# A hybrid decoder step whose opening is rewritten as one list of 370 steps over all engines

## The chip, the cores and the metric

The kernel runs on one core of a Trainium2 chip. The metric is the device time of one execution in microseconds (us), as the median over several runs. TensorE (PE) does matrix products and transposes into the accumulation banks of PSUM; VectorE (DVE), ScalarE (ACT) and GpSimd (POOL) work element by element; SyncE (SP) and ACT issue the transfers (DMAs) of this kernel, each on a queue of its own. Every engine works through its own list of instructions in order, and the engines wait for each other through semaphores.

## The reference, cut to what matters

One layer of a decoder: 1024 prompt rows and 8x8 sample rows, 1024 channels. Cut to the part that the opening of the kernel touches:

```
shift, scale, gate = jnp.split(jax.nn.silu(c) @ w_ada + b_ada, 3, axis=-1)
h = rmsnorm(x, norm_g) * (1 + scale[:, None]) + shift[:, None]
proj = h @ w_in
u_pool, z_pool, z_ssm, xbc, dt_raw, g_raw = jnp.split(proj, SPLITS, axis=-1)
dt = jax.nn.softplus(dt_raw + dt_bias)
gates = jax.nn.sigmoid(g_raw)
...
m = gates[..., :D_MODEL] * p + gates[..., D_MODEL:] * s
x = x + gate[:, None] * (m @ w_o)
```

Behind this follow a pooling branch, a state space branch (convolution, scan over chunks, gated norm), two output projections, and the final norm.

## The kernel before

**The whole.** h is kept transposed in SBUF, eight channel tiles k of 128 channels by T = 1088 columns (1024 prompt, 64 sample), as a high and a low part, `hh_[k]` (float32r) and `hl_[k]` (the rest), so that a product takes three matmuls: high by high, low weight by high, high weight by low. Most of w_in is multiplied in pairs of 128-column tiles by a seven-product Strassen-Winograd scheme (`strassen`, line 654, each product two halves of 12 matmuls 128x272). It needs sums of the h tiles (S1 to S4, made by `combine`, line 507, in place in `tf`) and of the weights (`pair_w`, line 556, through `split`, line 165: ACT writes `whi`, DVE or POOL writes `wlo`).

**The opening**, `first` (line 898), goes up to the end of the first such pair. The 1088 columns are taken as three blocks `BLK` of 256, 384 and 448 columns, made from x tiles 0-1, 2-4 and 5-8 (x tile 8 holds the 64 sample rows). For each block: load the x tiles; sum of squares of each (`x_square`, L204); a square root (L215) and a reciprocal (L219); `x_unit` (L224) scales an identity by it, and `x_spread` (L226) multiplies that by ones on PE, so that the row factors stand along columns in `rsb`; `x_turn` (L255) transposes each channel tile on PE, and `x_out` (L270) multiplies the transposed tile by `rsb` into `tf[k]`: for even k by DVE, for odd k by a copy on ACT (L275) and a multiply on POOL (L276). `c_silu`, `c_turn` and the `ada_...` functions (L299-L335) make shift and scale, in four parts p of two channel tiles each: 32 small matmuls (L305), a copy, a transpose (L320), and adds into `md`. `h_make` (L337) makes the two parts of h of one block from `tf` and `md`. `products` (L914) multiplies two tiles of gate columns (kept in `gs_d`, L924 the matmul) by block and by pairs of channel tiles; `dt_block` (L770) multiplies the dt columns; `gate_mm` (L879) the eight 512 KB rows of w_ada for gate. `warm(n)` (L246) puts n matmuls of ones on PE, whose results nobody reads.

**What sets the order.** `in_line` (L368) chains every instruction of each engine in the order in which the program writes it, for all five engines (SP with its loads among them). So the order inside `first` is the order of its calls; the tags and buffer numbers of the pools only add waits (a load into a buffer waits until its old content has been read). PE stands in it as follows: transposes of all three blocks, then from L924 on `products` in the order of blocks 0, 1, 2 for k = 0-1, then 2-3, 4-5, 6-7, with ada parts between; the gate rows 0-3 behind blocks 0 and 1 of the last k; the dt blocks; gate rows 4-7; then the fourteen half products of Strassen (L643). Behind the opening the units of the other pairs follow, with instructions placed by a scheduler.

Of the kernel before, what the change touches and what calls it, by code (L numbers as in the profile page):

```python
# [46 lines left out]
def tile_pool_ssd_step(  # L47
# [100 lines left out]
    def c_silu():  # L148
        act(c9, c9, AF.Silu)
        act(rs[:, 0:1], eps, AF.Sqrt)  # L150

    def c_turn():
        ps = PB()
        for k in range(KT):
            nc.tensor.transpose(ps[:, k * 9:k * 9 + 9], c9[:, k * P:(k + 1) * P], ident[:9, :9])
        V.tensor_copy(scT[:, :, 0:9], ps[:, :72].rearrange("p (k b) -> p k b", b=9))

    def v_turn():
        ps = PB()
        nc.tensor.transpose(ps[:, :44], vb, ident[:44, :44])  # L160
        V.tensor_copy(vT, ps[:, :44])
        V.tensor_scalar(vT[:, 8:16], vT[:, 8:16], 1.0, None, ALU.add)


# [25 lines left out]
    xr = []  # L190
# [8 lines left out]
    def x_load(i):  # L199
        n = P if i < 8 else NS  # L200
        xt = R([P, D]) if i == 8 else xbig[i // 4][:, i % 4, :D]
        load(xt[:n], x_prompt[0, i * P:(i + 1) * P, :] if i < 8 else x_sample.rearrange("b t d -> (b t) d"))
        xr.append((xt, n))

    def x_square(i, eng):
        xt, n = xr[i]
        sqj = pa.tile([P, D], F32, tag="rawA", name=nm("sqj"), bufs=3)
        if eng is V:
            V.scalar_tensor_tensor(sqj[:n], xt[:n], 1.0, xt[:n], ALU.mult, ALU.mult, accum_out=ss[:n, i:i + 1])
        else:  # L210
            act(sqj[:n], xt[:n], AF.Square, accum_out=ss[:n, i:i + 1])

    def x_root(a, b):
        n = xr[a][1]
        act(rs[:n, a:b], ss[:n, a:b], AF.Sqrt, bias=eps[:n], scale=1.0 / D)  # L215

    def x_unit(a, b):
        n = xr[a][1]
        V.reciprocal(rs[:n, a:b], rs[:n, a:b])  # L219
        if not dg:  # L220
            dg.append(R())
        for i in range(a, b):
            n = xr[i][1]
            V.tensor_scalar(dg[0][:n, i * P:i * P + n], ident[:n, :n], rs[:n, i:i + 1], None, ALU.mult)  # L224
# [3 lines left out]
    turns, turned = [0], []  # L228

    def x_spread(g3, eng):  # L230

        pr = PB()
        c = 0
        for i in range((0, *XG)[g3], XG[g3]):
            n = xr[i][1]
            mm(pr[:, c:c + n], ones[:n, :], dg[0][:n, i * P:i * P + n], start=True, stop=True)
            c += n
        o = BLK[g3][0]
        if eng is V:
            V.tensor_copy(rsb[:, o:o + c], pr[:, :c])  # L240
        else:
            act(rsb[:, o:o + c], pr[:, :c], AF.Copy)

    beat = []

    def warm(n):  # L246

        if not beat:
            beat.append(PC())
        for _ in range(n):  # L250
            mm(beat[-1][:, 256:256 + P], ones, ones, start=True, stop=True)

    def x_turn(g3, *ks):

        banks = []  # L255
        for k in ks:
            if g3 == 0:
                tf[k] = tfp.tile([P, T], F32, tag="tf", name=nm("tf"), bufs=8)
            banks.append((PA if turns[0] % 2 else PB)())
            turns[0] += 1  # L260
        c = 0
        for i in range((0, *XG)[g3], XG[g3]):
            xt, n = xr[i]
            for k, px in zip(ks, banks):
                nc.tensor.transpose(px[:, c:c + n], xt[:n, k * P:(k + 1) * P], ident[:n, :n])
            c += n
        turned.extend((g3, k, px, c) for k, px in zip(ks, banks))

    def x_out(n=1):
        for _ in range(n):  # L270
            g3, k, px, c = turned.pop(0)
            o = BLK[g3][0]
            t, r = tf[k][:, o:o + c], rsb[:, o:o + c]
            if k % 2:
                act(t, px[:, :c], AF.Copy)  # L275
                nc.gpsimd.tensor_tensor(t, t, r, ALU.mult)  # L276
            else:
                V.tensor_tensor(t, px[:, :c], r, ALU.mult)
# [20 lines left out]
    def ada_mm(part, k):  # L299
        a, b = PARTS[part]  # L300
        n = (b - a) * P // 2
        if k == 0:
            pm[part] = PC() if part else beat[0]
        for j in range(4):
            mm(pm[part][32 * j:32 * j + 32, :n], scT[:, k, :], wraw[part, k][:, j // 2, j % 2 * n:j % 2 * n + n],  # L305
               start=(k == 0), stop=(k == KT - 1))

    def ada_out(part):
        a, b = PARTS[part]
        n = (b - a) * P // 2  # L310
        mr = pa.tile([P, 256], F32, tag="rawA", name=nm("mr"), bufs=3)
        act(mr[:, :n], pm[part][:, :n], AF.Copy)
        return mr

    def ada_end(part, mr):
        a, b = PARTS[part]
        ni = (b - a) // 2
        ps = PB()
        for i in range(ni):
            nc.tensor.transpose(ps[:, i * P:(i + 1) * P], mr[:, i * P:(i + 1) * P], ident)  # L320
        pv = ps[:, :ni * P].rearrange("p (i j b) -> p j i b", i=ni, j=4)
        for s in (1, 0):
            m = slice(8 * s + a, 8 * s + b)
            V.tensor_tensor(md[:, m].rearrange("p (j i) b -> p j i b", i=ni), pv[:, 2 * s:2 * s + 2, :, 0:9],
                            vT[:, m].rearrange("p (j i) -> p j i", i=ni).unsqueeze(3).to_broadcast([P, 2, ni, 9]), ALU.add)
            if s:
                V.tensor_tensor(md[:, m], md[:, m],
                                vT[:, 16 + a:16 + b].unsqueeze(2).to_broadcast([P, b - a, 9]), ALU.mult)

# [6 lines left out]

    def h_make(g3, ks):  # L337

        o, w = BLK[g3]
        e = min(o + w, SEQ) - o  # L340

        def low(k):
            V.tensor_tensor(hl_[k][:, o:o + w], tf[k][:, o:o + w], hh_[k][:, o:o + w].bitcast(F32), ALU.subtract)
        for k in ks:
            if hh_[k] is None:
                hh_[k], hl_[k] = h_tile(k, 0), h_tile(k, 1)
            t = tf[k][:, o:o + w]
            hi = hh_[k][:, o:o + w]
            sc, sh = md[:, 8 + k], md[:, k]
            if e == w:  # L350
                act(hi, t, AF.Identity, scale=sc[:, 0:1], bias=sh[:, 0:1])
            if k % 2:
                act(t[:, :e], t[:, :e], AF.Identity, scale=sc[:, 0:1], bias=sh[:, 0:1])
            else:
                V.tensor_scalar(t[:, :e], t[:, :e], sc[:, 0:1], sh[:, 0:1], ALU.mult, ALU.add)
            if e < w:
                ts_ = t[:, e:w].rearrange("p (b i) -> p b i", i=8)
                V.tensor_tensor(ts_, ts_, sc[:, 1:9].unsqueeze(2).to_broadcast([P, NB, 8]), ALU.mult)
                V.tensor_tensor(ts_, ts_, sh[:, 1:9].unsqueeze(2).to_broadcast([P, NB, 8]), ALU.add)
# [1933 lines left out]
```

## Time and profile before

| | |
|---|---|
| median of three runs | 1270.49 us (1265.09 to 1270.58) |
| profiled execution | 1269.77 us |
| span of its trace, first to last instruction | 1268.1 us |
| mean granted TensorE clock over the span | 0.996 |
| PE busy in the span | 98% |
| DVE, POOL, ACT busy | 77%, 57%, 54% |
| the opening's PE work | from 1.07 us to about 105 us |

The profiled execution lies 0.72 us under the median, and its span 1.67 us under its own time. Rows of the profile are read so: a timeline row has the start in us, the duration, the engine, the line of the kernel, the operation, what it writes <- what it reads, the number of like instructions in a row, and in brackets how long the engine stood idle before it and what ended that. An fp32 matmul of the program stands as two or more in the trace. PEclk is the share of its full clock that TensorE was granted.

### The profile page before, as it was taken

How to read it: one execution, taken by the hardware profiler on the slowest of the kernel's cores; microseconds unless marked ns; L12 is line 12 of the kernel's file. 1: busy time of each engine (PE TensorE's matmuls, PEld its weight loads, DVE VectorE, ACT ScalarE, POOL GpSimd, SP SyncE). 2: the span in 40 equal slices, each digit the busy share in tenths (PEclk: the TensorE clock that was granted, in tenths of full speed). 3: DMA queues.
4: the chain of work that ended last, by engine and by line, in shares of the span. 5: the costliest groups of instructions: out<-in, count | busy, mean ns of one | idle time of the engine just before them, and what ended most of it. 6: DMA issues, size and time to landing. Idle time of an engine off the chain costs nothing.

```text
span 1268.1 us, 26648 instructions
## 1 busy us (share of the span) xinstructions
PE 1247.2 (98%) x9775; PEld 1164.8 (92%) x9775; DVE 978.2 (77%) x1715; ACT 682.3 (54%) x1570; POOL 727.5 (57%) x621
## 2 busy tenths in 40 slices
PE   9999999999999999999999999999999999999997
PEld 8779999999999999999989999998898888899885
DVE  5786689986998588876676775488687898659986
ACT  5665347465556546455655554645676655401425
POOL 4106767786868777764444444355686877503662
PEclk9999999999999999999999999999999999999999
DMA  9836454565546455444656565998888887766884
GB/s 323 248 134 207 148 158 149 183 199 162 162 157 197 161 156 176 132 148 121 175 168 192 175 184 156 317 317 266 254 247 284 285 242 256 267 215 218 250 194 155
DMA packets 264675, 257.99 MB, mean 203 GB/s; under 512 B 29889, under 2 KB 204561, under 8 KB 264538
## 3 DMA queue, kind: packets, MB, share of 16 engines
q1 hardware_dynamic: 183808, 163.93, 42.3%
q10 hardware_dynamic: 78434, 88.18, 20.1%
q0 software_dynamic: 2304, 4.20, 1.8%
q8 instruction: 77, 1.26, 0.4%
q14 instruction: 52, 0.43, 0.1%
HBM read 171.26 MB, written 85.10 MB: 202 GB/s over the span
## 4 chain that ended last, share of the span: by engine, by line
PE 65%; DVE 3%; DMA 2%; issue 1%; POOL 1%; ACT 1%; SPq 0%; ACTq 0%; POOLq 0%; DVEq 0%
PE mm L387 17%; PE mm L643 14%; PE ps L643 14%; PE ps L1284 2%; PE pc L643 2%; PE pc L1606 2%; PE ps L1287 2%; PE ps L2088 2%; PE ps L2090 2%; PE ps L2089 2%; DMA xb<-xbc 2%; PE ps L1581 1%; PE ps L1374 1%; PE ps L1397 1%; PE mm L2098 1%
## 5 line engine op out<-in xcount | busy, mean ns | idle before, releaser
L171 POOL TENSOR_TENSOR wlo<-rawA,whi 128x512 fp32r<-128x512 f32 x120 | 172.5, 1441 | 158.7 <-ACT whi L168 100.8
L171 POOL TENSOR_TENSOR wlo<-raw,whi 128x512 fp32r<-128x512 f32 x94 | 155.3, 1661 | 96.6 <-ACT whi L168 89.7
L387 PE MATMUL mm<-Y,whi 128*128 128x352 f32 (+1 forms) x960 | 197.2, 335 | 0.3 <-DVE Y L1644 0.3
L387 PEld LDWEIGHTS mm<-Y,whi 128*128 128x128 f32 x960 | 160.1, 189 | 6.6 <-issue 4.8
L1127 DVE SCALAR_TENSOR_TENSOR GA<-GA,cvT,GA 128x1112 f32<-128x1112 f32 x72 | 132.1, 1839 | 0.1
L643 PE MATMUL mm<-Y,whi 128*128 128x272 f32 x832 | 125.3, 292 | 3.0 <-ACT whi L168 2.1
L643 PE MATMUL ps<-Y,whi 128*128 128x272 f32 x832 | 123.3, 291 | 0.0
L168 ACT ACTIVATE whi<-raw 128x512 fp32r<-128x512 f32 x96 | 59.5, 628 | 109.8 <-DVE raw L575 48.6
L643 PEld LDWEIGHTS mm<-Y,whi 128*128 128x128 f32 x832 | 112.2, 188 | 6.2 <-ACT whi L168 2.2
L168 ACT ACTIVATE whi<-rawA 128x512 fp32r<-128x512 f32 x125 | 78.0, 626 | 72.9 <-PE ps L643 39.5
L643 PEld LDWEIGHTS ps<-Y,whi 128*128 128x128 f32 x832 | 111.8, 189 | 0.4
L1272 ACT ACTIVATE dec<-dec,acT 128x128 f32<-128x128 f32 (+1 forms) x288 | 86.9, 383 | 25.4 <-POOL dec L1263 24.3
L387 PE MATMUL mm<-Y,wlo 128*128 128x352 f32 (+1 forms) x480 | 99.4, 329 | 0.0
L387 PEld LDWEIGHTS mm<-Y,wlo 128*128 128x128 f32 x480 | 82.3, 189 | 0.0
L463 POOL TENSOR_TENSOR pw<-pw,ph 128x512 fp32r<-128x512 f32 x40 | 68.9, 1722 | 14.3 <-ACT ph L461 14.0
L643 PE MATMUL mm<-G,whi 128*128 128x272 f32 x496 | 73.6, 290 | 0.0
L643 PE MATMUL ps<-G,whi 128*128 128x272 f32 x496 | 72.6, 288 | 0.0
L643 PE MATMUL ps<-Y,wlo 128*128 128x272 f32 x416 | 69.6, 289 | 0.0
L643 PE MATMUL mm<-Y,wlo 128*128 128x272 f32 x416 | 69.5, 289 | 0.0
L643 PEld LDWEIGHTS mm<-G,whi 128*128 128x128 f32 x496 | 66.9, 189 | 0.7
L643 PEld LDWEIGHTS ps<-G,whi 128*128 128x128 f32 x496 | 66.3, 188 | 0.0
L1543 POOL TENSOR_TENSOR Y<-xb,Y 128x512 fp32r<-128x512 f32 x32 | 41.6, 1301 | 38.1 <-ACT Y L1541 38.1
(545 smaller groups left out, 3230.9 us busy)
## 6 DMA issues: line engine op xcount, KB each, us to landing
rawA<-in_w_in SPq DMA_DIRECT2D x62, 512.0 KB
dec<-acs_d SPq DMA_DIRECT2D x32, 512.0 KB
xbc<-GA ACTq DMA_DIRECT2D x24, 512.0 KB
Y<-wo SPq DMA_DIRECT2D x10, 1024.0 KB
pw<-in_w_ssm_out ACTq DMA_DIRECT2D x32, 256.0 KB
ws<-ph ACTq DMA_DIRECT2D x32, 256.0 KB
ws<-pw ACTq DMA_DIRECT2D x32, 256.0 KB
h<-in_state_ssm SPq DMA_DIRECT2D x32, 256.0 KB
```

The costliest lines, as they stand in the source:

```text
L168: ins = act(hi[:, :, :ncols], raw[:, :, :ncols], AF.Copy)
L171: (eng or nc.gpsimd).tensor_tensor(lo[:, :, :ncols], raw[:, :, :ncols], hi[:, :, :ncols].bitcast(F32), ALU.subtract)
L387: mm(ps[:, :n], w[k // 4][h][:, k % 4, :], r[k][:, o:o + n], start=(j == 0), stop=(j == len(terms) - 1))
L463: nc.gpsimd.tensor_tensor(raw.bitcast(F32R), raw, hi.bitcast(F32), ALU.subtract)
L643: mm(p, w[j // 8][:, k], A(k, s)[j // 4 == 1], start=(j == 0), stop=(j == 11))
L1127: V.scalar_tensor_tensor(d[:, :n], rp[:, k:k + n], cvT[:, 24 * k + mc:24 * k + mc + 1], d[:, :n], ALU.mult, ALU.add)
L1272: act(dec[:, h], dec[:, h], AF.Exp, bias=acT[:S, c, 8 * g + h:8 * g + h + 1], scale=-1.0)
L1284: mm(o[hh], xd[:S, 2 * q + hh, :], dec[:S, 2 * q + hh], start=True, stop=state is None)
L1287: mm(o[hh], state[:, h * 64:h * 64 + 64], cE[:, h], start=False, stop=True)
L1543: nc.gpsimd.tensor_tensor(yl[g][:, :, o:o + S], v, yhc.bitcast(F32), ALU.subtract)
L1606: mm(pu, bt, xw.rearrange("p h d -> p (h d)"), start=True, stop=True)
L2088: mm(ps, hi, y[:, k, c0:c0 + cw], start=(first and k == 0), stop=False)
```

## The change

The closures of the opening (`c_silu`, `c_turn`, `v_turn`, the `x_...`, `ada_mm`, `ada_out`, `ada_end`, `h_make`, `combine`, `gate_mm`, `gate_end`, and the early variants in `pair_w` and `strassen`) are gone. In their place `first` walks through `ORDER1`, a list of 370 words; each word is one step of one engine, with a letter where several engines could do it (V, A, G for DVE, ACT, POOL). `in_line` chains all five engines as before, and behind the opening the instructions stand in the order of before.

```
+    ORDER1 = """
+        warm6 sq0.A silu sq1.V turn0.0 turn0.6 turn0.7 turn0.5 turn0.2 cturn tab sq2.V vturn warm2 sct root0
+        sq8.V sq3.A turn0.1 warm8 unit0.V sq4.A vt spread0 root1 rsb0.A ada0.0 unit1.V ada0.2 out0.0 out0.1
...
+        pr0.6 t0.7.A wl1.V gt0 h2.7 l0.7.V gt2 wl0.V gt4 l1.6.V pr0.7 l2.6.V pr1.6 sgt ca2.V pr2.6 l2.7.V
...
+    """.split()
...
+        free, held, said = ["B", "A", "B", "A", "B", "A", "B"], {}, set()
+        def bank(key):
+            p = free.pop(0)
+            held[key] = (PA() if p == "A" else PB(), p)
+            return held[key][0]
...
+        def out(g, k):
+            o, w = BLK[g]
+            V.tensor_tensor(tf[k][:, o:o + w], give(("turn", g, k))[:, :w], rsb[:, o:o + w], ALU.mult)
...
+        def warm(n):
+            if pm[0] is None:
+                t = beat[0]
+            elif len(free) > 1:
+                t = bank("warm")
+                give("warm")
+            else:
+                return
...
+        def gt(k0):
...
+            for k in (k0 + 4, k0 + 5):
+                if k < KT:
+                    gate_load(k)
...
-        for i in range(9):
-            x_load(i)
+        x_load(8, store_)
...
+        for word in ORDER1:
...
+            calls[name](*args)
+            said.add(".".join(f for f in fs if f.isdigit() or f == fs[0]))
+            loads()
```

In words: the seven PSUM banks go round in a list, and a bank comes back when the step that reads it is written. The 24 `out` steps are one DVE multiply each (before: 12 on DVE, 12 as an ACT copy and a POOL multiply). Of the squares, DVE does x tiles 1, 2, 8 and 6 and ACT the rest (before: DVE 0, 1, 3, 5, 8). `warm` does nothing when fewer than two banks are free; 16 matmuls of the program are left of 43 written before. `pr b.k` is one channel tile k of block b (6 matmuls, before 12 for two tiles), from block 1 on. Loads come from a list that is emptied as far as its conditions are met. Their order on SP is x tiles 0-4, ada part 0, two weight tiles, x tiles 5-7, the other ada parts; x tile 8 goes on ACT's queue. Gate row k + 4 is loaded by the step that multiplies gate row k, into its buffer.

**ACT's first instructions.** R_116 holds c; vb the vectors b_ada, norm_g, ssm_norm_g, pool_scale; R_224 is x tile 8 (after); ss and rs the sums of squares and their roots. Before:

```order
L140 DMA vb<-in_norm_g 8x128
L141 DMA vb<-in_ssm_norm_g 16x128
L142 DMA vb<-in_pool_scale 4x128
L149 ACTIVATE R_116<-R_116 9x1024
L150 ACT_TABLE_LOAD
L150 ACTIVATE rs<-eps 128x1
L215 ACTIVATE rs<-ss,eps 128x2
```

After, in the same place:

```order
L140 DMA vb<-in_norm_g 8x128
L141 DMA vb<-in_ssm_norm_g 16x128
L142 DMA vb<-in_pool_scale 4x128
L185 DMA R_224<-in_x_sample 64x1024
L673 ACTIVATE sqj_279,ss<-Y_129 128x1024
L722 ACTIVATE R_116<-R_116 9x1024
L725 ACT_TABLE_LOAD
L725 ACTIVATE rs<-eps 128x1
L677 ACTIVATE rs<-ss,eps 128x2
```

The load of x tile 8 and the square of x tile 0 now stand ahead of silu (the ACTIVATE on R_116).

**DVE's first instructions after the change.** tf is h before shift and scale, vT the transposed vectors, R_339 the scaled identities, R_224 x tile 8.

```order
L671 SCALAR_TENSOR_TENSOR sqj_282,ss<-Y_129 128x1024
L671 SCALAR_TENSOR_TENSOR sqj_314,ss<-Y_129 128x1024
L733 COPY scT<-mm_304 128x8x9
L671 SCALAR_TENSOR_TENSOR sqj_322,ss<-R_224 64x1024
L681 RECIPROCAL rs<-rs 128x2
L688 TENSOR_SCALAR R_339<-ident,rs 128x128 x2
L739 COPY vT<-ps_316 128x44
L740 TENSOR_SCALAR vT<-vT 128x8
L681 RECIPROCAL rs<-rs 128x3
L688 TENSOR_SCALAR R_339<-ident,rs 128x128 x3
L718 TENSOR_TENSOR tf_284<-ps_285,rsb 128x256
```

The square of x tile 8 (R_224) has moved ahead of the first reciprocal; before it was DVE's seventeenth instruction, behind the multiplies of blocks 0 and 1.

**PE at the gate rows.** pc_963 (after: pc_919) is the accumulator, scT the transposed silu(c); the R and gk tiles are rows of w_ada. Before, rows 2 and 3 with their neighbours (rows 0 and 1, R_811 and R_813, stand one group of 12 products earlier, and rows 4 to 7 behind the dt blocks):

```order
L924 MATMUL mm_609<-G_930,whi_756 128x384
L924 MATMUL ps_610<-G_930,whi_760 128x384
L883 MATMUL pc_963<-R_815,scT 32x256 x4
L883 MATMUL pc_963<-gk_817,scT 32x256 x4
L924 MATMUL ps_674<-G_925,whi_756 128x448
```

After, rows 0 to 5 in one piece:

```order
L844 MATMUL ps_762<-G_868,whi_709 128x256
L882 MATMUL pc_919<-R_677,scT 32x256 x4
L882 MATMUL pc_919<-R_679,scT 32x256 x4
L882 MATMUL pc_919<-R_681,scT 32x256 x4
L882 MATMUL pc_919<-gk_827,scT 32x256 x4
L882 MATMUL pc_919<-R_928,scT 32x256 x4
L882 MATMUL pc_919<-R_930,scT 32x256 x4
L844 MATMUL mm_761<-G_871,whi_654 128x256
```

R_928 and R_930 (gate rows 4 and 5) take the buffers of R_677 and R_679 (rows 0 and 1), so that their loads start when PE has read those; between the last reading and the need stand the eight matmuls of rows 2 and 3.

783 lines of the change are left out of this document (351 added, 432 removed).

## The prediction

> **What bounds the kernel now.** I read the page first, then the waits of PE in the opening, then the timeline of PE, and then the rows of the engines that PE waits for. The page:
>
> ```profile
> span 1268.1 us, 26648 instructions
> PE 1247.2 (98%) x9775; PEld 1164.8 (92%) x9775; DVE 978.2 (77%) x1715; ACT 682.3 (54%) x1570; POOL 727.5 (57%) x621
> ```
>
> PE is idle for 21 us of the whole span, so the kernel ends when PE's work ends, and the opening matters as far as it lets PE start late or wait. The waits of PE up to 105 us (us in total, times, the longest):
>
> ```profile
> PE mm L643 <- ACT whi L168: 2.1, 1, 2.1
> PE mm L924 <- ACT G L351: 1.2, 2, 1.0
> ...
> PE mm L924 <- ACT Y L351: 1.0, 1, 1.0
> PE mm L643 <- DVE Y L513: 0.9, 2, 0.6
> ```
>
> These are what an order could take away: 5.2 us. The timeline of PE places them:
>
> ```profile
> 30.38 1.00 PE L924 MATMUL mm<-Y,whi 128*128 128x256 f32 x4 [0.97 <-ACT Y L351]
> ...
> 79.70 1.28 PE L643 MATMUL mm<-Y,whi 128*128 128x272 f32 x8 [2.13 <-ACT whi L168]
> ...
> 81.48 2.02 PE L643 MATMUL ps<-Y,whi 128*128 128x272 f32 x8
> ...
> 84.20 1.33 PE L643 MATMUL mm<-G,whi 128*128 128x272 f32 x8
> ...
> 85.88 1.17 PE L643 MATMUL ps<-G,whi 128*128 128x272 f32 x8
> ...
> 88.87 1.16 PE L643 MATMUL ps<-G,whi 128*128 128x272 f32 x8
> ...
> 90.38 1.16 PE L643 MATMUL mm<-Y,whi 128*128 128x272 f32 x8
> ...
> 106.85 1.18 PE L643 MATMUL ps<-G,whi 128*128 128x272 f32 x8
> ```
>
> The first product starts at 30.38; before it PE only has transposes, small matmuls and warm-up, and waits for DVE, ACT and POOL. The row at 106.85 is my mark: the first G product of the next pair, with all of the opening and two half products of that pair behind it, before and after the change. A half product takes 1.51 us (88.87 to 90.38), but the one at 79.70 took 1.78, the next 2.72 and the third 1.68. The windows say why:
>
> ```profile
> 77.70:81.10 3.40, 1.40 (x11) 1.40 (x12) 1.93 (x3) 2.59 (x6) 0.00 (x0) 1.00 0.18 65
> 81.10:84.50 3.40, 3.40 (x18) 3.40 (x17) 3.38 (x6) 2.64 (x6) 0.00 (x0) 0.50 0.18 67
> ```
>
> In the first stretch PE (first busy column) worked 1.40 of 3.40 us, and in the next its clock was 0.50. So the wait of 2.13 us cost a second time: 0.27 + 1.21 + 0.17 = 1.65 us.
>
> **The change part by part.** I follow PE from its first product to the mark. Before, this took 106.85 - 30.38 = 76.47 us, of which the waits behind the first product are 1.2 (G) + 2.13 + 0.9 = 4.2 and the half clock 1.65; PE's own work is 70.6 us. The sum after is: start of the first product, plus this work as it is now, plus new waits.
>
> *What is taken away, 5.9 us.* The products now stand by single tiles, the dt blocks and the rest of the products stand between the first Strassen halves, and the weights' high parts (`wh0`, `wh1`) are written some 25 words ahead of the first half that reads them. In the old order ACT's list has `whi` behind the copies of two dt blocks. I take all 4.2 us of waits and the 1.65 us of half clock as gone, and put 0.2 us of short new waits in their place.
>
> *Work that moves behind the first product, +0.25 us.*
>
> ```profile
> 15.38 0.27 PE L265 MATMUL ps<-ident,Y 128*128 128x128 f32 x1
> 15.49 0.27 PE L265 MATMUL mm<-ident,Y 128*128 128x128 f32 x1
> ...
> 21.68 1.30 PE L236 MATMUL ps<-R,ones 128*128 128x128 f32 x8
> ...
> 32.40 1.08 PE L305 MATMUL pc<-G,scT 128*32 128x128 f32 x32
> 33.41 0.45 PE L924 MATMUL mm<-Y,whi 128*128 128x384 f32 x1
> ```
>
> Four turns of block 2 with four transposes each come later: 16 x 0.11 = 1.75 us. Three quarters of ada part 1 (24 of the program's matmuls; 16 of them are the 32 of the row at 32.40, 1.01 us) come earlier: -1.5 us.
>
> *Warm-up, 0.* The program has 43 warm-up matmuls before and 16 after (twice that in the trace). All stand ahead of the first product, where PE waits for others anyway; nothing is gained. What they cover is the clock there; that is a bound below.
>
> *The start of the first product, +0.3 us.* This is DVE's chain now, since DVE has all 24 `out` multiplies. The rows of one group each:
>
> ```profile
> L276 POOL TENSOR_TENSOR tf<-tf,rsb 128x256 f32<-128x256 f32 (+2 forms) x12 | 12.0, 1018 | 15.3 <-ACT tf L275 12.4 <-DVE rsb L240 2.9
> L278 DVE TENSOR_TENSOR tf<-ps,rsb 128x256 f32<-128x256 f32 (+2 forms) x12 | 5.9, 528 | 0.4 <-ACT rsb L242 0.4
> L275 ACT ACTIVATE tf<-mm 128x256 f32<-128x256 f32 (+2 forms) x12 | 5.1, 467 | 0.0
> ```
>
> For 5.9 us more on DVE, POOL loses 12.0 and ACT 5.1. The chain starts with x tile 8, whose square stands ahead of everything on DVE:
>
> ```profile
> 4.91 1.23 DVE L209 SCALAR_TENSOR_TENSOR sqj<-Y 128x1024 f32<-128x1024 f32 x1 [4.91 <-DMA Y<-in_x_prompt]
> ...
> 6.30 1.23 DVE L209 SCALAR_TENSOR_TENSOR sqj<-Y 128x1024 f32<-128x1024 f32 x1 [0.16 <-DMA Y<-in_x_prompt]
> ...
> 8.74 0.48 DVE L224 TENSOR_SCALAR R<-ident,rs 128x128 f32<-128x128 f32 x2
> ...
> 10.42 1.49 DVE L278 TENSOR_TENSOR tf<-ps,rsb 128x256 f32<-128x256 f32 x4
> ...
> 15.44 1.49 DVE L278 TENSOR_TENSOR tf<-ps,rsb 128x384 f32<-128x384 f32 x3 [0.37 <-ACT rsb L242]
> 16.92 1.22 DVE L209 SCALAR_TENSOR_TENSOR sqj<-R 64x1024 f32<-64x1024 f32 x1
> ...
> 27.66 0.85 DVE L162 TENSOR_SCALAR vT<-vT 128x8 f32<-128x8 f32 x1
> ...
> 30.36 0.41 DVE L355 TENSOR_SCALAR tf<-tf,md 128x256 f32<-128x256 f32 x1 [0.67 <-ACT Y L351]
> 30.81 0.42 DVE L343 TENSOR_TENSOR Y<-tf,Y 128x256 fp32r<-128x256 f32 x1
> ```
>
> When does x tile 8 land? On ACT's queue it follows five small loads:
>
> ```profile
> 2.15 0.33 ACTq L140 DMA_DIRECT2D vb<-in_norm_g  x1
> ...
> 4.82 0.32 ACTq L141 DMA_DIRECT2D vb<-in_ssm_norm_g  x1
> 5.22 0.28 ACTq L142 DMA_DIRECT2D vb<-in_pool_scale  x1
> 5.55 1.06 ACT L149 ACTIVATE R<-R 9x1024 f32<-9x1024 f32 x1 [2.33 <-DMA R<-in_c_sample]
> ```
>
> The load issued at 4.82 followed one issued at 2.15, so issues are held up there by over 2 us; x tile 8 goes out between 5.5 and 8. The first x tile (512 KB) was there 4.1 us after its issue at 0.8, and the next 1.39 us later; with half the bytes at half the rate beside SP's loads it is 4.1 us again. So it lands between 9.6 and 12.1; from above I have only 16.92, where DVE reads it today without a wait. I take 12.0, by the held issue. Silu then starts not at 5.55 but behind that issue and a square, near 9, and scT is there at 11, which is ahead of 12.
>
> From 12.0 DVE has, up to the reciprocal of block 2: two squares 2.4; three reciprocals and md's three small steps, each at most an identity's 0.24, 1.3 in all; five scaled identities 1.2; vT 0.45 (its 0.85 of today stands beside a POOL multiply that goes; bounds 0.24, the identity's, and 0.85; I stay near the lower one); seven outs of 256 at 0.37 and six of 384 at 0.50, 5.6; a `wlo` of 512, 0.67 by the outs of 384; three scalings and three lows at 0.41 and 0.42 for 256, 0.55 for 384, 2.8. That is 14.4 us, to 26.4. Into it fall waits: identity, spread and ACT's copy follow each other across three engines, 0.65 + 0.47 for block 0 and 1.0 + 0.47 for block 1 (the row at 21.68 holds four identities' spread, 0.33 each; L275's mean for the copy), 2.6 together; vT covers 0.7 of it: 1.9, bounds 0 and 4. So 28.3. Then come four scaled identities on ACT (the first 0.47, then 0.25 each as DVE's) and the spread of block 2 (1.30) that stands ahead of the first product on PE: 2.4. The first product starts at 30.7, against 30.38. Bounds: 28 (x tile 8 at 9.6, vT and waits low) and 35.6 (x tile 8 at 16.92).
>
> *The gate rows, +3.5 us and a half clock of +1.35.*
>
> ```profile
> 50.53 1.30 SPq L877 DMA_DIRECT2D R<-in_w_ada  x3
> ...
> 61.01 1.07 PE L883 MATMUL pc<-R,scT 128*32 128x256 f32 x16
> ...
> 61.71 3.62 SPq L877 DMA_DIRECT2D R<-in_w_ada  x3
> ```
>
> Before, the loads of rows 4 and 5 went out from 61.71 on, when their buffers came free, and PE asked for them only behind the dt blocks. Now PE has rows 0 to 5 in one piece. Two rows take 1.0 us (61.01). The load of row 4 goes out 0.5 us after the start, when row 0 is read, and by the x tiles it lands 4.1 us later, at 4.6; PE is there at 2.05: a wait of 2.6. Row 5, a transfer of 1.39 later, costs 0.9 more: 3.5 us. Bounds: 1 (a landing in 2 us) and 5. Everything on PE behind gt4 waits with it: the products of the last tiles and the Strassen halves. By the windows at 77.70 an idle share like this halves the clock of the next 3.4 us; the second wait lies in that stretch, so (3.4 - 0.7) / 2 = 1.35, bounds 0 and 1.7.
>
> The Trainium skill has a rule on this, "TensorE: Matmul & The Clock Gate", Part 1 on the clock gate: the array falls to half clock after at least one idle window of about 3.4 us, counted freely from the kernel's start. The rows above disagree with it as it stands: PE was 41% busy in the stretch ahead of the one at 0.50. By the rule a wait of 2.6 us would leave the clock alone, and the sum would be 1.35 us less.
>
> **Sum.** Taken away 5.9; added 0.3 + 0.25 + 0.2 + 3.5 + 1.35 = 5.6. The mark moves by -0.3 us, from 106.85 to 106.5. Behind it the order is that of before and PE is the bound, so this goes to the end: 1269.77 - 0.3 = 1269.5 us by the profiled execution, which lies 0.72 under the median.
>
> **The rivals.**
>
> *The gate rows do not hold PE* (faster). If they land in about 2 us, or the first product is late enough that other work slides between, 3.5 + 1.35 do not come: 1264.6; with a first product at 28.5 as well, 1262.4. For it: DMA is nearly idle by then (share 0.18 in the rows at 77.70). Against: the 4.1 us of the first x tile were measured on an idle queue too.
>
> *x tile 8 is late* (slower). It sits on ACT's queue, and its issue also holds up what stands behind it on ACT: the square of x tile 0, silu, the first root. Each us after 12.0 moves the first product by a us, since DVE stands still in front of it; above 12.3 the kernel is slower than before. At 16.9 it is +4.9: 1274.4, and with one half-clocked stretch at the start of the products, since PE then idles before them with 27 warm-ups fewer, 1276. For it: in the old order nothing asked for x tile 8 before 16.92. Against: 256 KB alone on a queue.
>
> *The change does not do what it says.* The halves between products still wait for `whi` or for DVE's sums, since DVE has more to do: 2.13 + 1.65 come back, 1273.3. Against: DVE was full before as well (3.38 of 3.40 us from 81.10 on), and PE waited for it only 0.9.
>
> *The half clock does not come at the gate rows*, as the rule has it: 1268.1. Against: the row at 0.50.
>
> **How the numbers follow.** Forecast 0.45; gate rows in time 0.17; x tile 8 late 0.18; waits come back 0.10; no half clock 0.10. Predicted is the forecast, 1269.5 us. The range reaches to the faster rival at its full price and the slower one at its full price: 1262 to 1276. A measurement of this kernel can tell about 0.5%, 6.3 us. Faster by more needs the first rival with an early first product: 0.14. Slower by more needs x tile 8 at its upper bound together with a half clock or returned waits: 0.13. Within: 0.73.
>
> **What would show it.** Right: a wait of about 2.6 and one of about 0.9 us of PE for a DMA of w_ada at the gate rows; a clock of 0.5 behind it; no wait for `whi`; DVE's longest early wait for x_sample, ending near 12; the first product near 30.7; the mark near 106.5. Wrong: a first product beyond 33, gate rows without a wait, or PE waiting for DVE's sums in the Strassen halves.

## The result and the profile after

The kernel after the change took 1270.56 us (median of 22 runs, 1265.07 to 1273.98), the kernel before 1269.55 us (22 runs, 1263.14 to 1277.51): ratio 1.0006, 95% interval 0.9991 to 1.0021. That is no change; the medians differ by 1.0 us, inside the interval. (`ORDER1` holds 341 words, not the 370 of the title.) The profiled execution took 1269.22 us at a mean granted clock of 0.994 (before 1269.77 us at 0.996). The page of after:

```profile
span 1267.5 us, 26537 instructions
PE 1243.8 (98%) x9721; PEld 1161.0 (92%) x9721; DVE 974.5 (77%) x1719; ACT 680.9 (54%) x1565; POOL 719.5 (57%) x610
```

PE still is the bound, with 3.4 us less busy time. What it waits for up to 110 us after the change (us in total, times, the longest):

```profile
PE pc L882 <- DMA R<-in_w_ada: 3.2, 2, 2.6
PE ps L713 <- DMA Y<-in_x_prompt: 2.8, 3, 1.0
PE pc L753 <- POOL ones L118: 1.1, 1, 1.1
PE ps L713 <- DVE md L778: 0.8, 1, 0.8
PE mm L730 <- ACT R L722: 0.8, 1, 0.8
PE pc L763 <- DMA G<-in_w_ada: 0.4, 1, 0.4
PE ps L696 <- DVE vT L739: 0.3, 1, 0.3
```

No wait for `whi` or for DVE's sums is left; of these rows only the first (gate rows) and the 0.4 us for an ada part lie behind the first product. The first row is new: the gate rows wait for their loads. The same in PE's timeline:

```profile
24.73 0.33 PE L713 MATMUL ps<-ident,Y 128*128 128x128 f32 x1 [1.03 <-DMA Y<-in_x_prompt]
...
27.24 2.79 PE L763 MATMUL pc<-G,scT 128*32 128x128 f32 x48
29.95 1.64 PE L696 MATMUL mm<-R,ones 128*128 128x128 f32 x8
31.52 0.45 PE L844 MATMUL mm<-Y,whi 128*128 128x384 f32 x1
...
59.27 1.50 PE L882 MATMUL pc<-R,scT 128*32 128x256 f32 x24
60.59 0.61 PE L882 MATMUL pc<-gk,scT 128*32 128x256 f32 x8
63.81 0.64 PE L882 MATMUL pc<-R,scT 128*32 128x256 f32 x8 [2.61 <-DMA R<-in_w_ada]
65.07 1.08 PE L882 MATMUL pc<-R,scT 128*32 128x256 f32 x8 [0.62 <-DMA R<-in_w_ada]
66.08 0.58 PE L844 MATMUL mm<-G,whi 128*128 128x256 f32 x1
...
71.10 0.67 PE L989 MATMUL mm<-Y,wlo 128*128 128x272 f32 x4
...
105.73 1.17 PE L413 MATMUL ps<-G,whi 128*128 128x272 f32 x8
```

The first product starts at 31.52 (before 30.38), and the mark, the first G product of the next pair, stands at 105.73 (before 106.85). Gate rows 0 to 3 run without a pause to 61.2; row 4 waits 2.61 us, row 5 0.62 us. Windows of after, laid so that two of them are the stretches of half clock (length; busy time of PE, PEld, DVE, ACT, POOL with counts; then granted clock, DMA share, GB/s):

```profile
23.90:27.30 3.40, 2.57 (x18) 1.68 (x22) 3.40 (x10) 3.15 (x8) 0.00 (x0) 1.00 1.09 347
27.30:30.70 3.40, 3.40 (x52) 2.85 (x52) 2.23 (x6) 1.00 (x4) 0.00 (x0) 0.50 1.10 349
61.40:64.80 3.40, 0.64 (x8) 0.16 (x8) 3.40 (x6) 0.00 (x0) 0.00 (x0) 1.00 0.96 366
64.80:68.20 3.40, 3.13 (x17) 2.32 (x18) 2.73 (x5) 0.38 (x1) 0.00 (x0) 0.50 0.70 266
```

One stretch follows the wait of the gate rows, as predicted. The other stands right ahead of the first product, where none was predicted. DVE and then ACT at the start, for x tile 8 (R) and c's silu (L722):

```profile
12.95 1.22 DVE L671 SCALAR_TENSOR_TENSOR sqj<-R 64x1024 f32<-64x1024 f32 x1 [2.53 <-DMA R<-in_x_sample]
```

```profile
6.38 0.56 ACTq L185 DMA_DIRECT2D R<-in_x_sample  x1
6.98 1.06 ACT L673 ACTIVATE sqj<-Y 128x1024 f32<-128x1024 f32 x1 [3.76 <-DMA vb<-in_b_ada]
8.03 1.04 ACT L722 ACTIVATE R<-R 9x1024 f32<-9x1024 f32 x1
```

x tile 8 is issued at 6.38, held up as expected, and DVE waits 2.53 us for it, until 12.95.

**Where PE's time went.** From the first product to the mark PE took 76.47 us before and 74.21 after. Summed by kind of instruction, each from its start to the start of the next one on PE:

```
                                     before   after   difference
products of the gate columns (144)    29.38   25.63     -3.75
Strassen halves (192)                 27.15   24.49     -2.66
transposes at 77 us, with the
  wait for whi that follows them       2.61    0.36     -2.25
ada parts                              6.06    5.39     -0.67
dt blocks                              7.34    7.47     +0.13
gate rows                              3.84    7.79     +3.95
16 transposes of x, block 2            0       2.72     +2.72
three transposes at the ada's end      0.08    0.37     +0.29
```

That is -2.24 us; with the first product 1.14 us later the mark is 1.1 us earlier.

### The profile page after: what moved, and what is told of

Its sections match the earlier page's. It is cut to its first block, busy times and chain, and to the rows that moved or that the text cites. A ratio compares the mean times of both kernels' runs of the same rounds, so it can differ in the third digit from the quotient of the medians.

```text
span 1267.5 us, 26537 instructions
## 1 busy us (share of the span) xinstructions
PE 1243.8 (98%) x9721; PEld 1161.0 (92%) x9721; DVE 974.5 (77%) x1719; ACT 680.9 (54%) x1565; POOL 719.5 (57%) x610
## 4 chain that ended last, share of the span: by engine, by line
PE 64%; DVE 3%; DMA 3%; issue 1%; POOL 1%; ACT 1%; SPq 0%; ACTq 0%; DVEq 0%; POOLq 0%
PE mm L238 16%; PE mm L413 14%; PE ps L413 14%; PE ps L1265 2%; PE pc L413 2%; PE pc L1587 2%; PE ps L1268 2%; PE ps L2069 2%; PE ps L2071 2%; PE ps L2070 2%; PE ps L1355 1%; PE ps L1562 1%; PE ps L1378 1%; DMA out<-xb 1%; PE pc L1369 1%
## 5 line engine op out<-in xcount | busy, mean ns | idle before, releaser
L154 POOL TENSOR_TENSOR wlo<-rawA,whi 128x512 fp32r<-128x512 f32 x120 | 176.4, 1475 | 155.0 <-ACT whi L151 141.7
L154 POOL TENSOR_TENSOR wlo<-raw,whi 128x512 fp32r<-128x512 f32 x90 | 149.5, 1670 | 86.0 <-ACT whi L151 76.7
L238 PEld LDWEIGHTS mm<-Y,whi 128*128 128x128 f32 x960 | 160.2, 189 | 6.6 <-issue 4.6
L413 PE MATMUL mm<-Y,whi 128*128 128x272 f32 x800 | 120.3, 292 | 0.0
L413 PE MATMUL ps<-Y,whi 128*128 128x272 f32 x800 | 117.9, 289 | 0.0
L151 ACT ACTIVATE whi<-rawA 128x512 fp32r<-128x512 f32 x120 | 75.3, 628 | 76.8 <-PE ps L413 42.4
L151 ACT ACTIVATE whi<-raw 128x512 fp32r<-128x512 f32 x90 | 55.8, 628 | 111.3 <-DVE raw L367 48.5
L413 PEld LDWEIGHTS mm<-Y,whi 128*128 128x128 f32 x800 | 107.9, 188 | 2.7 <-issue 0.9
L413 PEld LDWEIGHTS ps<-Y,whi 128*128 128x128 f32 x800 | 106.6, 188 | 0.8 <-issue 0.4
L413 PE MATMUL mm<-Y,wlo 128*128 128x272 f32 x400 | 66.7, 288 | 0.0
L413 PE MATMUL ps<-Y,wlo 128*128 128x272 f32 x400 | 66.5, 288 | 0.0
```

Source lines behind the costliest of these rows:

```text
L151: ins = act(hi[:, :, :ncols], raw[:, :, :ncols], AF.Copy)
L154: (eng or nc.gpsimd).tensor_tensor(lo[:, :, :ncols], raw[:, :, :ncols], hi[:, :, :ncols].bitcast(F32), ALU.subtract)
L238: mm(ps[:, :n], w[k // 4][h][:, k % 4, :], r[k][:, o:o + n], start=(j == 0), stop=(j == len(terms) - 1))
L413: mm(p, w[j // 8][:, k], A(k, s)[j // 4 == 1], start=(j == 0), stop=(j == 11))
```

## The experiments

**The theory** was the prediction's: the new order does take the old waits away, and the gate rows, whose next load cannot start before PE has read the buffer, give nearly all of it back, by their wait and by the half clock behind it. The rivals: the old waits could have been had by one moved step; or the first product, now late, is what counts. For the late first product there were three readings: DVE's chain behind x tile 8, the landing of the x tiles, and the half clock at 27. Each ratio below is to the kernel before, by the runs of the same call; "mark" and "first product" are of the profiled execution, one for each kernel. Four kernels have the same order up to the first product (after, experiments 1 and 2, and in experiment 6 the first of the two with other buffers), and it starts at 31.52, 31.41, 31.20 and 32.71 in them; a difference within these 1.5 us is not put down to an edit.

### 1. The gate rows' second turn later

```diff
- ... l0.7.V gt2 wl0.V gt4 l1.6.V ...
+ ... l0.7.V gt2 wl0.V l1.6.V ...
- ... dto2 gt6 cc1.V ...
+ ... dto2 gt4 gt6 cc1.V ...
```

> The changed kernel with the multiplication of gate rows 4 and 5 (gt4) moved from behind gt2 to just ahead of gt6, 20 us later; nothing else. Theory (the stall at the gate rows and its half clock are what the change gives back): the two PE waits of 2.61 and 0.62 us go, the clock stays at 1.0 from 60 to 70 us, the mark (first G product of the next pair) comes 4.5 us earlier, near 101.2 instead of 105.73, and the time falls by 4 to 5 us, 0.35%. Rival (DVE is the bound behind the gate rows, it was busy throughout the stall): the products of the last tiles wait for DVE's lows instead, the mark comes at most 1.5 us earlier and the time is the same.

Measured: 1266.08 us, ratio 0.9979 (0.9960 to 0.9998). PE in this kernel:

```profile
60.56 0.61 PE L882 MATMUL pc<-gk,scT 128*32 128x256 f32 x8
61.11 0.38 PE L844 MATMUL mm<-G,whi 128*128 128x256 f32 x1
...
76.64 1.48 PE L882 MATMUL pc<-R,scT 128*32 128x256 f32 x24
...
101.12 1.17 PE L413 MATMUL ps<-G,whi 128*128 128x272 f32 x8
```

Behind rows 0 to 3 the products go straight on, rows 4 to 7 run without a wait at 76.64, and there is no half clock in the sixties. The mark is 4.61 us earlier than after's, where the stall was priced at 4.85. At the mark the theory held; the time fell by 2.6 us in the medians, not by the 4 to 5 expected (more on that behind the experiments).

### 2. The half clock alone: the wait filled

Eleven matmuls of ones, read by nobody, between rows 0-3 and row 4: the wait stays, PE is busy in it.

```diff
+        def fill(n):
+            t = bank("fill")
+            give("fill")
+            for _ in range(n):
+                mm(t[:, 256:256 + P], ones, ones, start=True, stop=True)
- ... gt2 wl0.V gt4 ...
+ ... gt2 wl0.V fill11 gt4 ...
```

> The changed kernel with eleven matmuls of ones put on PE between gt2 and gt4, 2.4 us in the wait for gate row 4; their results are not read. The wait for the load stays. Theory (the idle share of a stretch of 3.4 us halves the clock of the next, apart from the wait itself): the clock stays at 1.0 from 63 to 70 us and the mark comes 1.2 to 1.6 us earlier, near 104.3. Rival (the half clock costs nothing there, since the products behind the gate rows wait for DVE anyway, or it comes all the same): the mark stays within 0.4 us of 105.73.

Measured: 1269.52 us, ratio 1.0011 (0.9994 to 1.0027); mark 104.61. PE (this kernel's lines stand 6 lower):

```profile
60.95 2.72 PE L759 MATMUL mm<-ones 128*128 128x128 f32 x22
63.82 0.64 PE L888 MATMUL pc<-R,scT 128*32 128x256 f32 x8 [0.15 <-DMA R<-in_w_ada]
65.08 0.64 PE L888 MATMUL pc<-R,scT 128*32 128x256 f32 x8 [0.62 <-DMA R<-in_w_ada]
...
69.72 0.67 PE L995 MATMUL mm<-Y,wlo 128*128 128x272 f32 x4
```

Rows 4 and 5 start where they did (63.82 and 65.08, after 63.81 and 65.07), so the landing sets them. The clock stays at 1.00, and from row 5 to the low half of the first Strassen product it is 4.64 us, in after 71.10 - 65.07 = 6.03: the half clock cost 1.39 us, with 1.35 predicted. The mark moved by 1.12, since the first product stood 0.32 earlier and 0.6 us went elsewhere on the way.

### 3. The old wait alone: one step moved in the kernel before

```diff
         dt_block(dtw, 0)
+        next(wst)
         dt_block(dtw, 1)
         next(sums)
-        next(wst)
         dt_block(dtw, 2)
```

> The kernel before with one call moved: the step that writes the first high and low weights of the Strassen pair stands ahead of the second dt block instead of behind it. Theory (the wait of 2.13 us for whi and the half clock after it are most of what the change takes away): the wait goes, the clock stays at 1.0 from 80 to 90 us, the mark comes 3.8 us earlier, near 103.1 instead of 106.85, and the time falls by 3 to 4 us, 0.3%. Rival (ACT and DVE are full there, and the wait only moves): PE waits as long for a sum of DVE or for the next weights a little later, and the mark stays within 1 us of 106.85.

Measured: 1270.77 us, ratio 1.0017 (1.0002 to 1.0032); mark 106.18. PE:

```profile
77.40 1.28 PE L643 MATMUL mm<-Y,whi 128*128 128x272 f32 x8
...
84.33 1.26 PE L643 MATMUL mm<-G,whi 128*128 128x272 f32 x8 [0.60 <-ACT whi L168]
...
92.48 1.28 PE L643 MATMUL mm<-Y,whi 128*128 128x272 f32 x8 [1.72 <-ACT whi L168]
```

The first half product starts at 77.40 in place of 79.70, and the half clock behind it is gone. But the wait turns up at the fifth and at the ninth half product (0.60 and 1.72 us), and the mark moves by 0.67 only, as the rival said. One moved step shifts the wait; the whole list is what takes it away.

### 4. The first product: is it DVE's chain?

Two kernels. In the first the square of x tile 8 stands behind the identities of block 1 on DVE, so that its landing holds nothing up; in the second half of the `out` steps (odd k) are again a copy on ACT and a multiply on POOL, as before the change.

```diff
-        sq8.V sq3.A turn0.1 ...
+        sq3.A turn0.1 ...
- ... unit1.V ada0.2 out0.0 ...
+ ... unit1.V sq8.V ada0.2 out0.0 ...
```

> The changed kernel with the square of x tile 8 moved on DVE from ahead of the first reciprocal to behind the identities of block 1; its load stays where it is. Theory (the wait of 2.53 us for x tile 8 sets the first product): the wait goes, the first product comes 2.3 to 2.5 us earlier, near 29.2 instead of 31.52, and the mark too, near 103.4. Rival one (loads set what follows: PE waits for rows of w_ada): the first product comes earlier by about 2 us, but the mark by under 1 us, with PE waits for DMA of w_ada between 25 and 45. Rival two (x tile 5, for which PE waited until 24.73, and the half clock from 26.8 on set the first product): it stays within 0.5 us of 31.5 and the mark of 105.7.

Measured: 1269.52 us, ratio 1.0000 (0.9985 to 1.0015); first product 32.59, mark 106.24. PE:

```profile
24.62 0.47 PE L713 MATMUL ps<-ident,Y 128*128 128x128 f32 x1 [1.04 <-DMA Y<-in_x_prompt]
...
28.70 2.73 PE L763 MATMUL pc<-G,scT 128*32 128x128 f32 x48
...
32.59 0.44 PE L844 MATMUL mm<-Y,whi 128*128 128x384 f32 x1
```

DVE's wait for x tile 8 is gone, and yet the first product is not earlier. DVE itself gains little, 0.28 us: its first `out` starts at 15.82, in after at 16.10, since it now waits for ACT's roots. PE waits for the same x tile as in after (24.62, there 24.73); then its turns take 4.08 us for 2.51, since here the half clock lies from 24.4 to 31.2.

```diff
-            V.tensor_tensor(tf[k][:, o:o + w], give(("turn", g, k))[:, :w], rsb[:, o:o + w], ALU.mult)
+            px, t, r = give(("turn", g, k))[:, :w], tf[k][:, o:o + w], rsb[:, o:o + w]
+            if k % 2:
+                act(t, px, AF.Copy)
+                nc.gpsimd.tensor_tensor(t, t, r, ALU.mult)
+            else:
+                V.tensor_tensor(t, px, r, ALU.mult)
```

> The changed kernel with the out steps of odd k as before the change: a copy on ACT and a multiply on POOL, at the same places of the list. Theory of the prediction (DVE, with all 24 outs, is the bound from 13 to 29 us): the first product comes 1 to 2 us earlier, near 30. Rival (x tile 7 and PE set it, DVE has slack): it stays within 0.5 us of 31.5. Third (DVE is slowed by POOL and ACT's own list gets longer: its squares and high parts come later): the first product comes more than 1 us later, beyond 32.5, and the mark too.

Measured: 1271.69 us, ratio 1.0016 (0.9998 to 1.0033); first product 31.70, mark 105.75. With half of DVE's `out` work gone the first product is not earlier. So it is not DVE's chain that sets it; this run shows that better than the one ahead of it. PE's own rows agree: the last wait that they list ahead of the first product is the one for an x tile, until 24.73 in after.

### 5. The first product: half clock or loads?

`warm` may use the bank of ada part 1 as well, so that ten warm-up matmuls of the program that after leaves out come back:

```diff
-            if pm[0] is None:
+            if pm[1] is None:
```

> The changed kernel with a warm-up that may also run between ada parts 0 and 1 (on the bank of part 0, which is free then): ten matmuls of ones stand again on PE ahead of the turns of block 2, near 22.5 us, where PE waits 0.84 us for a bank and 1.03 us for x tile 7. Nothing else. Theory (the first product is set by PE itself: x tile 7 lands at 24.7, and then PE's transposes, ada part 1 and the spread run at half clock from 27.3 to 30.7): the half clock goes, the first product comes 1.2 to 1.6 us earlier, near 30.1 instead of 31.5, and the mark near 104.4 instead of 105.73. Rival (the chain of DVE sets the first product): it stays within 0.3 us of 31.5, half clock or not.

Measured: 1270.99 us, ratio 1.0020 (1.0002 to 1.0037); first product 30.74, mark 106.03. PE:

```profile
28.41 0.43 PE L763 MATMUL pc<-G,scT 128*32 128x128 f32 x8 [0.18 <-DMA G<-in_w_ada]
29.16 0.43 PE L763 MATMUL pc<-G,scT 128*32 128x128 f32 x8 [0.32 <-DMA G<-in_w_ada]
...
30.74 0.44 PE L844 MATMUL mm<-Y,whi 128*128 128x384 f32 x1
```

The half clock at 27 is gone and the first product is 0.78 us earlier. That is outside the spread: the four kernels with these warm-ups (this one and three of experiment 6) start it at 30.61 to 30.93, the four without at 31.20 to 32.71. The rest of the half clock's price goes to waits for the loads of the ada parts, 1.5 us in five places (after: 0.4), 0.5 of it ahead of the first product. And the gain does not reach the mark: PE comes to the gate rows at 59.27 as in after, and behind their wait the half clock now starts at 65.9 and lies wholly on work.

The other way round, x tiles 5 to 7 are loaded ahead of ada part 0:

```diff
-("x04", "p0", "w", "x57", "p1", "p2")
+("x07", "p0", "w", "p1", "p2")
```

> The changed kernel with x tiles 5 to 7 loaded right behind x tile 4, ahead of ada part 0 and the first two weight tiles, as in the order before; nothing else. Theory one (the wait for x tile 7 until 24.7 sets the first product): PE's waits for x tiles near 23 to 24.7 go and the first product comes 1 to 2 us earlier, near 30. Theory two (the same 6.75 MB have to land ahead of the first product in any order): what comes later now, ada part 0 and the weight tiles, makes PE and ACT wait instead, and the first product stays at 31 to 33, the mark within 1 us of 105.73.

Measured: 1270.16 us, ratio 1.0005 (0.9987 to 1.0023); first product 31.80, mark 106.34. PE in the opening:

```profile
PE ps L713 <- DMA Y<-in_x_prompt: 2.2, 2, 1.4
...
PE pc L763 <- DMA Y<-in_w_ada: 1.2, 4, 0.3
```

PE now waits for ada part 0 (1.2 us in four places) and a little less for the x tiles (2.2 us for 2.8). What goes first saves a wait and what goes last gains one. With the windows above (DMA share 1.09 and 1.10, about 348 GB/s) the reading that fits both runs is that the bytes which must land by then set the first product, with PE's turns and ada products behind the last x tile; a kernel with fewer bytes there was not tried.

### 6. What limits once the gate stall is gone

Experiment 1 with experiment 4's late square, and then with the warm-up of experiment 5:

> Both edits, gt4 late and the square of x tile 8 late. If they are independent, the mark moves by the sum of the two: near 99 by the first theory of each, near 100.5 if the loads of w_ada hold the second back, and the time falls by 5 to 7 us, 0.4 to 0.5%. If DVE bounds the stretch behind 60 us, the earlier arrival is eaten up there and the mark stays above 102.

Measured: 1266.78 us, ratio 0.9973 (0.9952 to 0.9993); first product 31.96, mark 101.09. Beside experiment 1 the mark is the same, so the late square does nothing here.

> gt4 late and the warm-up between ada parts 0 and 1. If the two causes are independent, the mark comes at 105.73 - 4.6 - 1.4, near 99.7, and the time falls against the kernel before by about 4 to 6 us, 0.4%. If the earlier start only meets the loads of w_ada, the mark stays near 101.

Measured: 1270.34 us, ratio 1.0012 (0.9991 to 1.0033); first product 30.67, mark 104.55. The first product is 0.74 us earlier than in experiment 1 and the mark 3.43 later. PE, and then ACT, in this kernel:

```profile
95.71 0.39 PE L989 MATMUL mm<-Y,whi 128*128 128x272 f32 x1 [1.32 <-DVE Y L658]
```

```profile
70.34 0.40 ACT L1005 ACTIVATE s<-mm 128x272 f32<-128x272 f32 x1 [5.91 <-DMA gs<-g]
```

PE waits 1.32 us for DVE's low part at the seventh product, and a half clock follows at 96.7. The reading was that DVE is late because ACT stood 5.91 us (in experiment 1 4.43) in front of a copy into the buffer "s1": the sigmoid of the first gate columns lies in it until it is stored. So the buffer of that sigmoid was changed, on experiment 1 and on experiment 6:

```diff
- tag=("s1", "u2", "u3", "c2")[2 * b + t]
+ tag=("u2", "u3", "u3", "c2")[2 * b + t]
```

> gt4 late, and the sigmoids of the first gate block kept in the buffers u2 and u3 instead of s1 and u2, so that the copy of the first Strassen half into s1 does not wait for their store to memory. Theory (with the gate stall gone, that store holds ACT for 4.4 us and DVE behind it, and PE has almost no slack against DVE's lows at the seventh product): ACT's wait for the store goes, DVE works 2 to 3 us earlier from 70 us on, PE waits nowhere behind the first product, and the mark stays at 101.1 as with gt4 late alone, since PE did not wait there either; the time is 0.2 to 0.5% below the kernel before. Rival (ACT stands still for another transfer or buffer): DVE is not earlier.

Measured: 1267.28 us, ratio 0.9980 (0.9965 to 0.9996); first product 32.71, mark 102.64. ACT's wait for the store is gone, but against what was expected PE waits 1.3 us for DVE at the seventh product, and the first product is later, with the half clock from 25.7 on for 6.8 us.

> gt4 late, the warm-up between ada parts 0 and 1, and the sigmoids of the first gate block in the buffers u2 and u3. Theory (in the run with the first two alone the store of a sigmoid held ACT for 5.9 us, DVE came late, PE waited 1.3 us for it at the seventh product and then ran at half clock for 3.4 us): wait and half clock go, and the mark comes at 100.4 to 101.1 instead of 104.55. Rival (PE is ahead of DVE's own work, not of a store): PE waits for DVE near 94 us again and the mark stays above 103.

Measured: 1267.76 us, ratio 0.9994 (0.9976 to 1.0012); first product 30.61, mark 102.05. No half clock comes in the opening, but PE's wait at the seventh product stays, 1.28 us. So the store did hold DVE (the four sums below start at 85.38, in experiment 6's second kernel at 87.78), but its end alone does not end PE's wait. DVE ahead of it:

```profile
85.38 3.73 DVE L658 TENSOR_TENSOR tf<-tf,tf 128x544 f32<-128x544 f32 x4
89.03 1.89 DVE L658 TENSOR_TENSOR Y<-tf,Y 128x544 fp32r<-128x544 f32 x1
```

The four sums took 3.73 us (2.63 in experiment 1) and the low part 1.89 (0.72 there), while POOL was at work from 86.87 on. In the kernel that follows, where POOL begins at 87.34, the sums took 2.62 and the same low part 0.72, but two later ones 3.27 together. Last, the low part that PE waits for was put ahead:

```diff
- u3.0 s4l2.V s4l0.G u4.0 m5.0 u3.1 lc s4l3.V m5.1
+ u3.0 s4l2.V s4l0.G s4l3.V u4.0 m5.0 u3.1 lc m5.1
```

> The run with gt4 late, the warm-up and the sigmoids in u2 and u3, and in addition the low part of the last S4 tile (s4l3) moved on DVE from behind the sums of the fourth and fifth product to right behind s4l2. Theory (PE's wait of 1.3 us at the seventh product is for s4l3, which stands too late in DVE's list): the wait goes, and the mark comes at 100.5 to 101 instead of 102.05; the time is 0.3 to 0.5% below the kernel before. Rival (DVE is full up to there whatever the order, slowed beside POOL): PE waits for a sum of DVE elsewhere, at the fifth to seventh product, and the mark stays above 101.7.

Measured: 1267.24 us, ratio 0.9981 (0.9963 to 0.9999); first product 30.93, mark 101.07. PE's wait for DVE is gone, as the reading of DVE's order asked. No version beat experiment 1 and the first kernel of experiment 6 at the mark by more than 0.05 us, nor in time by more than the intervals allow.

## Why the prediction was right

The time was forecast as nearly unchanged, 1269.5 us, and the mark as 0.3 us earlier; measured were 1269.22 us in the profiled execution and 1.1 us. That the two fit so well is in part luck: the sum held because three sizes were off in opposite directions.

*What is taken away* (predicted 5.9 us less 0.2 of new waits): right in kind, 9.6 us in size. Halves (-2.66) and the wait for `whi` (-2.25) came as priced. The gate columns' products did not: in experiment 1, where no half clock falls on them, they take 24.65 us, 4.73 less than before, and the wait list had put 1.2 down for them. The other 3.5 us are pauses that the list does not show as waits, or only in part. (An estimate: at the closest spacing in after, 0.12, 0.17 and 0.20 us for the three widths, 48 matmuls of each take about 23.5 us; before took 29.38.) PE before, three groups of four matmuls of one size:

```profile
58.99 0.99 PE L924 MATMUL mm<-G,whi 128*128 128x256 f32 x4 [0.19 <-ACT G L351]
59.82 0.63 PE L924 MATMUL mm<-G,wlo 128*128 128x256 f32 x4
60.29 0.79 PE L924 MATMUL mm<-G,whi 128*128 128x256 f32 x4
```

From start to start the first takes 0.83 us, the second 0.47 and the third, up to the gate row at 61.01, 0.72; only the first names a releaser, with 0.19. The step that failed is to take PE's time behind the first product as work plus listed waits.

*Work that moves* (+0.25): measured +2.47 (2.72 + 0.29 + 0.13 - 0.67). Sixteen transposes cost 0.17 us each there, and not the 0.11 of the rows that were read. Those rows are of block 1; in block 2 the kernel before took 1.07 us for eight from 23.70 on, 0.13 each. What makes the rest of the difference is open: it is not the bank alone, since three into one bank followed each other by 0.11 us in after, at 18.02. And the ada products saved 0.67 for 1.5.

*The first product* (+0.3): +1.14, and for another reason. x tile 8 landed at 12.95, outside the 9.6 to 12.1 that were given (6.57 us behind its issue; the reasons for a late issue held, the 4.1 us of transfer did not), and DVE waited for it as said. But DVE's chain does not set the first product (experiment 4), and that step of the prediction failed. In the reading that fits experiment 5 the loads do, with PE's turns and ada products behind them, in part at half clock; this is argued, not shown.

*Warm-up, 0*: wrong. With 27 warm-ups fewer the clock fell at 27.3. Experiment 5 gives the worth of ten of them as 0.78 us at the first product; the loads take the rest.

*The gate rows* (+3.5 and +1.35): right. The waits were 2.61 and 0.62 us, predicted 2.6 and 0.9, and the half clock 1.39. Row 4 landed 3.84 us behind its issue at 59.97, for which 4.1 had been taken. Experiment 1 shows both parts together, experiment 2 the half clock by itself. The Trainium skill, "TensorE: Matmul & The Clock Gate", Part 1, lets the clock fall after at least one idle window (free-running, so not started by the kernel); here PE was busy for 0.64 of the 3.40 us ahead of the fall, and the rival built on that rule (no half clock, 1268.1) is out.

Of the rivals, x tile 8 was late by 0.95 us without deciding anything, and the waits for `whi` and for the sums did not come back.

**Behind the mark.** The difference to before, followed through PE's instructions (us, negative is earlier):

```
at (us of before)        111     641     664     828    1027    1138    1240
after                  -1.12   -1.05   -2.65   -1.40   +0.15   -0.29   -0.29
gate rows later (1)    -5.74   -5.72   -4.27   -2.85   -2.18   -3.71   -3.71
both (6, first)        -5.77   -5.75   -7.29   -5.88   -5.07   -7.05   -7.05
low part ahead (6, last) -5.58 -5.14   -3.34   -1.77   +2.51   +0.50   +0.50
```

For 530 us the lead is passed on, unchanged in three rows and less 0.44 us in the fourth; then it jumps, by up to 4.3 us, either way. At 640 to 650 the jump can be read. Experiment 1, in windows laid by its half clock, and then before, in a window laid by its own half clocks (they start at 81.1 and 1122.2, 305 windows apart by this count, and 647.7 is the 166th from the first):

```profile
641.30:644.70 3.40, 1.61 (x12) 1.53 (x12) 2.24 (x10) 1.78 (x5) 1.29 (x1) 1.00 0.86 262
644.70:648.10 3.40, 3.40 (x17) 3.40 (x16) 0.62 (x3) 0.63 (x1) 0.00 (x0) 0.50 0.85 217
```

```profile
647.70:651.10 3.40, 2.21 (x16) 2.16 (x17) 1.83 (x8) 1.63 (x4) 1.29 (x1) 1.00 0.78 241
```

PE waits once for ACT's `s` there in both, 1.79 us in experiment 1 and 1.84 us before (in after 0.25, which is its jump of -1.6). In experiment 1 the wait and shorter pauses leave PE 1.61 us of the window, and 3.4 us at half clock follow; before, it was busy for 2.21 us of its window, and nothing follows. So 1.45 us of the lead are lost by where an old wait falls. The largest of the later jumps can be read as well: in the version with the low part ahead PE waits 2.80 us for DVE's `xw`, until 1020.97, where before it does not wait; PE is busy for 0.77 of the 3.40 us up to 1020.80, and 3.4 us at half clock follow. A lead of 1.01 us becomes a lag of 3.52 there. None of these jumps was followed up by an experiment. Why the versions with a lead of 5.7 us at the mark gain only 2.4 to 3.4 us by their ratios (1.9 to 2.9 in the medians) stays open to that extent.

## What to carry to other kernels

A load into a buffer that PE must read first belongs a whole transfer ahead of its use: with two rows of other work between, the wait was 3.23 us and the half clock behind it another 1.39, together 4.6 of the 5.7 us that the rewritten order leads by at the mark without them. Price a reordering by the time from start to start of each kind of instruction, not by the list of waits: here the list missed 3.5 of 9.6 us. And a gain of 5 us in the opening of a kernel like this must be shown over many runs, since waits that were there before can hand over 1.5 us each, either way, by where they fall against the clock's windows.

## What the runs showed of the hardware

- The half clock comes in stretches of 3.4 us (or 6.8), after stretches in which PE did matmuls for 0.64, 1.40 and 1.61 of 3.40 us, and once 1.97 (experiment 6, second kernel, 93.30 to 96.70); after 2.21 us it did not come, nor after 2.13 (experiment 6, the first of the two with other buffers, 93.97 to 97.38).
- The stretch ahead of after's half clock at 27.3 had PE busy for 2.57 us, and yet the clock fell. The same window of after, and the one ahead of it, for L713 alone, the transposes against the identity (length; PE and PEld busy with counts; clock, DMA share, GB/s):

```profile
20.50:23.90 3.40, 2.03 (x12) 1.31 (x12) 1.00 1.02 379
23.90:27.30 3.40, 2.57 (x14) 1.61 (x14) 1.00 1.09 347
```

All of the busy time of the second is theirs. The Trainium skill, "TensorE: Matmul & The Clock Gate", Part 4 on the PE-mode transpose, says that transposes do not count as busy in the same way. The stretch at 23.90 agrees, and so does the first kernel of experiment 4, where the late turns stand in a half clock of 6.8 us. The stretch at 20.50 does not: PE was busy for 2.20 us there, with these turns and one transpose of L771, and the clock stayed at 1.00 behind it. So it stays open how much a transpose counts; no run here took the transposes apart from the rest.
- At the start the pace and the clock column differ: in after the turns at 7.31 follow each other by 0.21 us and those at 18.02 by 0.11, and the column says 1.00 for both. In before, with more warm-ups, the pace of 0.11 us is there from 6.6 us on.
- x tile 8, 256 KB on ACT's queue beside the loads of SP, took 6.57 us from issue to DVE's start on it; the first x tile, 512 KB and ahead of all others on SP's queue, 4.1 us.
- DVE's TENSOR_TENSOR of 128x544 took 0.72 us as a rule and up to 1.89 us in stretches in which POOL worked too. In the last kernel of experiment 6 it is the other way round: DVE's low part took its 0.72 us, and POOL's instruction beside it 3.97, against 1.65 in the kernel ahead of it. That the two hinder each other is the reading; it was not tried by itself.
- Over the 116 runs of the kernel before that stand beside the experiments the time goes with the mean granted clock, with a correlation of -0.73.
